# A cast queued behind a copy in the third feed-forward layer, and a pause ahead of the first state update in the linear attention

## The chip, the cores and the metric

The kernel runs on one core of a Trainium2 chip. The core has a matrix engine (PE, with PEld for its weight loads), a vector engine (DVE), a scalar engine (ACT), a general engine (POOL) and a synchronisation engine (SP) that here only issues transfers; POOL issues transfers too. Each engine works through its own queue of instructions in order, and semaphores hold an instruction back until what it needs is done. The metric is the time of one execution in microseconds (us).

## The reference

A trunk of four layers on 512 tokens of 1024 features, in fp32. Each layer is a mixer and a feed-forward network (FFN), each behind an RMS norm and added to the residual. The mixers are a state-space scan, a gated linear attention, a differential attention and the scan again. What matters here:

```python
def swiglu_ffn(h, w_gate_up, w_down):
    g, u = jnp.split(h @ w_gate_up, 2, axis=-1)
    return (jax.nn.silu(g) * u) @ w_down

# gla_mixer, chunks of 64 tokens, 4 heads
upd = jnp.einsum('bnchk,bnchv->bnhkv', k_dec, v)
decay = jnp.exp(tot)
def chunk_step(state, xs):
    dec_c, upd_c = xs
    state = dec_c[..., None] * state + upd_c
    return state, state
...
o = jnp.einsum('bnchk,bnhkv->bnchv', q, states)
o = o * lax.rsqrt(jnp.mean(o * o, axis=-1, keepdims=True) + NORM_EPS) * norm_g
```

The hidden width of the FFN is 2816.

## The kernel before

**Precision.** Each fp32 matrix is kept as a high part (a cast to fp32r on ACT, L420) and a low part (what the cast left, on DVE, L428); a product is three matmuls, high by high, high by low and low by high. The pair of a weight tile is `whl`, of which five exist; a new cast waits until the product that read the oldest pair is through.

**Seven products.** The gate-up matrix is worked in 11 blocks of 256 columns of each half (`b` 0 to 10). A block multiplies two 2 x 2 arrangements of quarters, and does so with seven products in place of eight. On the weight side the quarters are "11", "21" and "22", the sum "1" (quarters 12 + 11, to which "22" is added for product six and "21" for product four) and the sum "3" (quarters 12 + 22). The sums "1" and "3" are made by two loads: a plain one that SP issues, and an accumulating one that POOL issues behind it. The tiles of "11" and "3" come from a pool of three (`wst`). The order on PE in a block is product one (PSUM bank `a`), five (bank `c`), six (on top of `a`), two (bank `d`), seven (on top of `a`), three (on top of `c`), four (on top of `a`), 24 matmuls each (L594). Between them ACT copies a bank out before the next product adds to it: L796 (`one_out`, tile `r1`), L814 (`five_out`, tile `r5`), L828 (`six_out`, tile `r2`); DVE adds and subtracts (L803, L834, L841, L842), multiplies with the norm's factors (L768) and by the gate (L851); ACT takes the silu (L769) and casts the result to the activation pair (L861, low part on DVE, L862). L817 adds quarters into "1".

The blocks go in groups of four, four and three, and behind each group stands the down product (L448 to L450, evicted at L576). The first two blocks of a layer are interleaved by a written plan and have their "3" split early. From block 2 on, product seven splits "3" when it is emitted, through the helper `halves`. The layer index of the third FFN is 2, and it alone is built with `turn`, since its activations leave in the order that the scan behind it wants.

**Linear attention.** Its input projection is done in six such blocks. Blocks 0 and 1 are interleaved. From block 2 on, `block` takes a list of steps and runs one behind each of the seven products. With block 3 these are `later` (exponents of the suffix sums, `suf`) and then `core(0)`: for the first two heads, `updates` (L2261, eight matmuls into two banks, then copies or state steps on DVE, L2269 and L2271) and `readout` (L2284, eight matmuls; squares with their sum on ACT, L2290; epsilon on DVE, `ms`, L539; the root on POOL, `rs`, L541; the scaled output on DVE, L2298). A step of `core` holds a readout and the next pair of updates; the last holds a readout alone. Block 4 carries `core(1)` for the other two heads.

**What sets the order.** In the linear attention from block 2 on, PE keeps the written order and the other queues are ordered when the kernel is built, by the builder's scheduler. In the third FFN behind the first two blocks all queues are ordered by it. `issue_after(x)` gives the scheduler one more rule, without a semaphore: what is written inside it, and runs on the engine of `x`, is queued behind `x`.

## Time and profile before

| | us |
|---|---|
| median of three runs | 2259.27 |
| lowest and highest | 2256.43, 2262.32 |
| the profiled execution | 2255.34 |
| its span, from the first to the last instruction | 2253.6 |

The span is 1.7 us shorter than the profiled execution's own time. In the profile's rows a time is given from the start of the span. A row of the timeline has the start, the length, the engine, the line, the operation, the tile written and the tiles read, the shape and how many such instructions are merged; in brackets stands the idle time before it and what ended it. An instruction's length can overlap its neighbour's, so the spacing of starts is what counts for an engine that works without a gap. A matmul's tile is named without its number: `a`, `c` and `d` are the PSUM banks above, `op` a readout, `upd` an update, `work` the state.

### The profile page before, as it was taken

What the parts mean: (1) busy time and instruction counts of PE and PEld (TensorE: products, weight loads), DVE (VectorE), ACT (ScalarE), POOL (GpSimd) and SP (SyncE); (2) the same over time, 40 slices, a digit from 0 to 9 for tenths busy, and PEclk for the clock granted to TensorE, in tenths of its full rate; (3) what the DMA queues carried; (4) which work ended last, traced back from release to release, by engine and by line L of the source; (5) the groups of instructions that cost most, each with busy time, mean ns of one, the idle gap of its engine ahead of it and who ended that gap; (6) DMA issues with size and microseconds to landing.
All of it is one profiled execution on the core that took longest, in us unless ns stands there. A gap on an engine that the chain in (4) does not pass through costs nothing.

```text
span 2253.6 us, 38448 instructions
## 1 busy us (share of the span) xinstructions
PE 2174.0 (96%) x15415; PEld 1969.4 (87%) x15415; DVE 1637.0 (73%) x2495; ACT 1137.2 (50%) x1827; POOL 338.1 (15%) x447
## 2 busy tenths in 40 slices
PE   6999999999999999999999999999999899999998
PEld 5888979989988899999888888989998788989997
DVE  9955878786877598776745676967766965957675
ACT  8534645444655365564435775644444234635443
POOL 4301141431211010100002221101000000101000
PEclk9999999999999999999999999999999999999999
DMA  4356666774863667765337465975641546766632
GB/s 90 63 170 160 168 168 172 175 182 133 207 149 94 168 161 198 178 175 135 103 128 163 97 143 143 251 196 133 180 99 48 157 143 157 197 161 161 167 75 75
DMA packets 309180, 333.62 MB, mean 148 GB/s; under 512 B 70477, under 2 KB 253033, under 8 KB 308874
## 3 DMA queue, kind: packets, MB, share of 16 engines
q1 hardware_dynamic: 238970, 238.93, 35.0%
q0 software_dynamic: 70032, 92.23, 21.9%
q8 instruction: 121, 1.98, 0.4%
q14 instruction: 57, 0.47, 0.1%
HBM read 297.16 MB, written 18.75 MB: 140 GB/s over the span
## 4 chain that ended last, share of the span: by engine, by line
PE 79%; DVE 9%; ACT 5%; issue 4%; DMA 2%; SPq 1%; POOL 1%; DVEq 0%; POOLq 0%; ACTq 0%
PE a L594 20%; PE acc L448 11%; PE acc L450 11%; PE acc L449 11%; PE c L594 10%; PE d L594 5%; PE y L1620 2%; DVE whl L428 2%; ACT whl L420 1%; PE op L2586 1%; PE s L2553 1%; DMA wst<-in_ffn_w_down_dram 1%; PE tp L117 1%; PE V L1584 1%; PE acc L2641 1%
## 5 line engine op out<-in xcount | busy, mean ns | idle before, releaser
L428 DVE TENSOR_TENSOR whl<-wst,whl 128x1024 fp32r<-128x1024 f32 x260 | 316.8, 1223 | 217.0 <-ACT whl L420 214.3
L420 ACT CAST whl<-wst 128x1024 fp32r<-128x1024 f32 x260 | 272.1, 1051 | 264.8 <-PE acc L450 176.1
L594 PE MATMUL a<-side,whl 128*128 128x256 f32 x3240 | 392.1, 277 | 9.1 <-DVE whl L428 6.3
L594 PEld LDWEIGHTS a<-side,whl 128*128 128x128 f32 x3240 | 378.5, 188 | 11.8 <-DVE whl L428 7.4
L448 PE MATMUL acc<-whl,act 128*128 128x512 f32 x704 | 276.0, 392 | 2.0 <-DVE g L768 2.0
L449 PE MATMUL acc<-whl,act 128*128 128x512 f32 x704 | 274.4, 390 | 0.0
L450 PE MATMUL acc<-whl,act 128*128 128x512 f32 x704 | 274.4, 390 | 0.0
L594 PE MATMUL c<-side,whl 128*128 128x256 f32 x2160 | 260.9, 277 | 3.8 <-DVE whl L428 3.8
L594 PEld LDWEIGHTS c<-side,whl 128*128 128x128 f32 x2160 | 252.6, 188 | 4.7 <-DVE whl L428 4.6
L428 DVE TENSOR_TENSOR whl<-slot,whl 128x1024 fp32r<-128x1024 f32 x105 | 127.7, 1221 | 66.4 <-ACT whl L420 65.9
L448 PEld LDWEIGHTS acc<-whl,act 128*128 128x128 f32 x704 | 132.1, 188 | 31.3 <-DVE g L768 2.9
L450 PEld LDWEIGHTS acc<-whl,act 128*128 128x128 f32 x704 | 132.1, 188 | 27.7
L420 ACT CAST whl<-slot 128x1024 fp32r<-128x1024 f32 x105 | 110.0, 1052 | 90.8 <-PE acc L450 46.2
L449 PEld LDWEIGHTS acc<-whl,act 128*128 128x128 f32 x704 | 132.2, 188 | 26.1
L594 PE MATMUL d<-sides,whl 128*128 128x256 f32 x1080 | 132.3, 278 | 2.5 <-ACT whl L420 2.5
L594 PE MATMUL a<-sides,whl 128*128 128x256 f32 x1080 | 132.3, 278 | 1.9 <-DVE whl L428 1.2
L420 ACT CAST whl<-halves 128x1024 fp32r<-128x1024 f32 x87 | 91.3, 1053 | 83.9 <-DVE halves L817 33.6
L594 PEld LDWEIGHTS d<-sides,whl 128*128 128x128 f32 x1080 | 127.8, 188 | 3.3 <-ACT whl L420 3.3
L594 PEld LDWEIGHTS a<-sides,whl 128*128 128x128 f32 x1080 | 127.9, 188 | 3.2 <-DVE whl L428 1.4
L428 DVE TENSOR_TENSOR whl<-halves,whl 128x1024 fp32r<-128x1024 f32 x87 | 105.9, 1220 | 32.2 <-ACT whl L420 31.9
L759 POOL DMA_DIRECT2D wst<-in_ffn_w_gate_up_dram x44 | 57.2, 1299 | 437.9 <-DMA wst<-in_ffn_w_gate_up_dram 206.2
L861 ACT CAST act<-r 128x512 fp32r<-128x512 f32 (+1 forms) x110 | 66.2, 644 | 104.6 <-DVE r L842 84.1
(496 smaller groups left out, 4066.3 us busy)
## 6 DMA issues: line engine op xcount, KB each, us to landing
wst<-in_ffn_w_gate_up_dram SPq DMA_DIRECT2D x88, 512.0 KB, 4.7
wst<-in_ffn_w_down_dram SPq DMA_DIRECT2D x88, 512.0 KB, 4.5
slot<-in_ffn_w_gate_up_dram SPq DMA_DIRECT2D x69, 512.0 KB, 6.9
wst<-in_ffn_w_gate_up_dram POOLq DMA_DIRECT2D x44, 512.0 KB, 6.1
halves<-in_ffn_w_gate_up_dram SPq DMA_DIRECT2D x42, 512.0 KB, 6.3
wst<-in_s_w_glu_dram SPq DMA_DIRECT2D x32, 512.0 KB, 4.9
wst<-in_diff_w_qkv_dram SPq DMA_DIRECT2D x24, 512.0 KB, 4.4
slot<-in_ffn_w_gate_up_dram POOLq DMA_DIRECT2D x18, 512.0 KB, 9.3
```

The costliest lines, as they stand in the source:

```text
L117: tr.nc.tensor.transpose(p[:, j], h[:, j * P : (j + 1) * P], tr.ident[:])
L420: self.last["high"] = self.nc.scalar.copy(hl[:, 0], w[:])
L428: self.last["low"] = self.nc.vector.tensor_tensor(hl[:, 1], w[:], hl[:, 0].bitcast(F32), op=ALU.subtract)
L448: mm(out, lh, rh, start=first, stop=False)
L449: mm(out, lh, rl, start=False, stop=False)
L450: self.last["mm"] = mm(out, ll, rh, start=False, stop=last)
L594: mm(o, *two, start=first and not (j or k or n), stop=k == 3 and n == 2, skip_group_check=True,)
L759: nc.gpsimd.dma_start(w[:], left.quarter(*plus, b), accum_op=ALU.add)
L861: self.last["act high"] = nc.scalar.copy(dst[:, 0, j], src[:, j])
L1584: mm(V[kk][z][:, bs(b)], inm[:, z, bs(b)], U[:, bs(b)], start=True, stop=True)
L1620: mm(yb[:, b], q[:, j, b], om[:, j // 2, bs(b)], start=False, stop=j == 3)
L2553: nc.tensor.matmul(ss[m][:], qs[:, m, ts], ks[:, m, z], start=z == 0, stop=z == 1)
```

## The change

Two edits, of which neither adds or removes arithmetic.

In `five_out` the copy of bank `c` is remembered. In `seven`, for the layer with `turn` and where "3" is not split yet, the cast of "3" is written inside `issue_after` that copy, and the low part behind it; `product` then finds the pair ready. The cast can so no longer stand ahead of its block's L814 on ACT.

In the linear attention an empty step is put between `later` and `core(0)`, so each step of the first two heads' core stands one product later. The first updates stood behind product five and now stand behind six; the first readout, with the second updates, stood behind six and now stands behind two; and so on to the last readout, which stood behind three and now stands behind four.

```diff
         def five_out():
             keep["r5"] = T("r5")
-            nc.scalar.copy(keep["r5"][:], bank["c"][:])
+            keep["tie"] = nc.scalar.copy(keep["r5"][:], bank["c"][:])
...
         def seven():
+            if turn and "3" not in H:
+                with self.tc.issue_after(keep["tie"].ins):
+                    high("3")
+                low("3")
             product("3", "3", bank["a"], False)
...
             vs[1] = room("D", "v1")
-            block(3, Rows(vs[1]), (later, *core(0)))
+            block(3, Rows(vs[1]), (later, pause, *core(0)))
```

The queues, first ACT in the third FFN around block 3 (the last of the first group). Its tiles are `r1_15076`, `r5_15106` and `r2_15136`; `whl_15169` is the pair of "3", `whl_15197` that of "22", `whl_15227` that of "1" for product four, and `act_15030` belongs to block 2. Before:

```order
L420 COPY whl_15139<-halves_14131 128x1024
L769 ACTIVATE g2_15026<-g2_15026 128x512
L420 COPY whl_15169<-wst_15045 128x1024
L796 COPY r1_15076<-a_15048 128x512
L861 COPY act_15030<-r5_14865 128x64x4 x2
L420 COPY whl_15197<-gain_13547 128x1024
L814 COPY r5_15106<-c_15078 128x512
L420 COPY whl_15227<-halves_14131 128x1024
L828 COPY r2_15136<-a_15048 128x512
```

and in the change (its lines from 831 on have numbers higher by 4):

```order
L420 COPY whl_15139<-halves_14131 128x1024
L769 ACTIVATE g2_15026<-g2_15026 128x512
L796 COPY r1_15076<-a_15048 128x512
L865 COPY act_15030<-r5_14865 128x64x4 x2
L814 COPY r5_15106<-c_15078 128x512
L420 COPY whl_15169<-wst_15045 128x1024
L420 COPY whl_15197<-gain_13547 128x1024
L420 COPY whl_15227<-halves_14131 128x1024
```

The cast of "3" moves from the place ahead of L796 to the place behind L814, and with the cast of "22" and that of "1" it makes three casts in a row.

The same queue in a later block, 5, whose tiles are `r1_15780`, `r5_15810` and `r2_15840`; `whl_15873` is the pair of "3". Before:

```order
L420 COPY whl_15873<-wst_15749 128x1024
L769 ACTIVATE g2_15730<-g2_15730 128x512
L796 COPY r1_15780<-a_15752 128x512
L420 COPY whl_15901<-halves_14131 128x1024
L861 COPY act_15734<-r5_15582 128x64x4 x2
L814 COPY r5_15810<-c_15782 128x512
L420 COPY whl_15931<-slot2_14311 128x1024
L828 COPY r2_15840<-a_15752 128x512
```

and in the change:

```order
L769 ACTIVATE g2_15730<-g2_15730 128x512
L796 COPY r1_15780<-a_15752 128x512
L865 COPY act_15734<-r5_15582 128x64x4 x2
L814 COPY r5_15810<-c_15782 128x512
L420 COPY whl_15873<-wst_15749 128x1024
L420 COPY whl_15901<-halves_14131 128x1024
L420 COPY whl_15931<-slot2_14311 128x1024
```

Here too the three casts follow each other behind L814, and L828 follows them as before.

PE in block 3 of the linear attention, from product five on (`c_6867`; six, seven and four write `a_6821`). Before:

```order
L594 MATMUL c_6867<-whl_6868,side1_6010 128x256 x24
L2261 MATMUL upd_6897<-v0_6013,kd_6549 128x256
L2261 MATMUL upd_6898<-v0_6013,kd_6549 128x256
L2261 MATMUL upd_6897<-v0_6013,kd_6549 128x256
L2261 MATMUL upd_6898<-v0_6013,kd_6549 128x256
L594 MATMUL a_6821<-whl_6908,side2_6011 128x256 x24
L2284 MATMUL op_6937<-work_6503,qT_6017 64x256 x4
L2261 MATMUL upd_6950<-v0_6013,kd_6549 128x256
L2261 MATMUL upd_6951<-v0_6013,kd_6549 128x256
L2261 MATMUL upd_6950<-v0_6013,kd_6549 128x256
L2261 MATMUL upd_6951<-v0_6013,kd_6549 128x256
L594 MATMUL d_6960<-whl_6961,sides_5772 128x256 x24
```

and in the change:

```order
L594 MATMUL c_6867<-whl_6868,side1_6010 128x256 x24
L594 MATMUL a_6821<-whl_6898,side2_6011 128x256 x24
L2265 MATMUL upd_6927<-v0_6013,kd_6549 128x256
L2265 MATMUL upd_6928<-v0_6013,kd_6549 128x256
L2265 MATMUL upd_6927<-v0_6013,kd_6549 128x256
L2265 MATMUL upd_6928<-v0_6013,kd_6549 128x256
L594 MATMUL d_6937<-whl_6938,sides_5772 128x256 x24
L2288 MATMUL op_6967<-work_6503,qT_6017 64x256 x4
L2265 MATMUL upd_6980<-v0_6013,kd_6549 128x256
L2265 MATMUL upd_6981<-v0_6013,kd_6549 128x256
L2265 MATMUL upd_6980<-v0_6013,kd_6549 128x256
L2265 MATMUL upd_6981<-v0_6013,kd_6549 128x256
```

Product six moves ahead of the first updates, and product two ahead of the first readout. On POOL the first root stays ahead of one accumulating load and the other roots behind it, as before.

## The prediction

> **What bounds the kernel now.** I read the page first, then the chain that ended last, then the timelines of the two places that the change touches.

> ```profile
> span 2253.6 us, 38448 instructions
> PE 2174.0 (96%) x15415; PEld 1969.4 (87%) x15415; DVE 1637.0 (73%) x2495; ACT 1137.2 (50%) x1827; POOL 338.1 (15%) x447
> ```

> TensorE is busy for 96% of the span. An edit of order can therefore gain only where PE waits at the two places, and it can lose wherever it makes PE wait. The first place is block 3 of the linear attention. Its PE rows, with the wait in brackets:

> ```profile
> 661.38 1.14 PE L2261 MATMUL upd<-v,kd 64*128 64x256 f32 x8
> ...
> 665.39 1.08 PE L2284 MATMUL op<-work,qT 128*64 128x256 f32 x8
> 666.40 1.13 PE L2261 MATMUL upd<-v,kd 64*128 64x256 f32 x8
> ...
> 670.47 1.83 PE L2284 MATMUL op<-work,qT 128*64 128x256 f32 x8
> 672.23 1.13 PE L2261 MATMUL upd<-v,kd 64*128 64x256 f32 x8
> ...
> 676.31 0.65 PE L2284 MATMUL op<-work,qT 128*64 128x256 f32 x2
> 679.36 1.08 PE L2284 MATMUL op<-work,qT 128*64 128x256 f32 x6 [2.40 <-DVE work L2271]
> 680.36 1.13 PE L2261 MATMUL upd<-v,kd 64*128 64x256 f32 x8
> ...
> 684.45 0.65 PE L2284 MATMUL op<-work,qT 128*64 128x256 f32 x2
> 685.83 1.08 PE L2284 MATMUL op<-work,qT 128*64 128x256 f32 x6 [0.73 <-DVE work L2271]
> 686.83 3.09 PE L594 MATMUL a<-whl,side 128*128 128x256 f32 x24
> ...
> 692.68 1.13 PE L2261 MATMUL upd<-v,kd 64*128 64x256 f32 x8
> ```

> A readout (`op`) that waits for nothing takes 1.01 from its start to the next row (665.39 to 666.40). The next three take 1.76, 4.05 and 2.38, so they lose 0.75, 3.04 and 1.37, together 5.16 us. They wait for the state steps of DVE (L2271), and DVE waits in its turn for POOL:

> ```profile
> 668.44 0.16 DVE L539 TENSOR_SCALAR ms<-ms 128x2 f32<-128x2 f32 x1
> ...
> 669.51 0.87 DVE L2298 SCALAR_TENSOR_TENSOR on<-op,rs,ng 128x256 f32<-128x256 f32 x2 [0.52 <-POOL rs L541]
> ...
> 677.64 0.88 DVE L2298 SCALAR_TENSOR_TENSOR on<-op,rs,ng 128x256 f32<-128x256 f32 x2 [3.71 <-POOL rs L541]
> 678.44 1.25 DVE L2271 SCALAR_TENSOR_TENSOR work<-work,dec,upd 128x256 f32<-128x256 f32 x3
> ...
> 688.00 0.16 DVE L539 TENSOR_SCALAR ms<-ms 128x2 f32<-128x2 f32 x1
> ...
> 689.87 0.88 DVE L2298 SCALAR_TENSOR_TENSOR on<-op,rs,ng 128x256 f32<-128x256 f32 x2 [0.58 <-POOL rs L541]
> ```

> On POOL the second root (L541) stands behind an accumulating load, and that one waits for a plain load, which the chain names:

> ```profile
> 675.54 1.33 POOL L626 DMA_DIRECT2D wst<-in_gla_w_in_dram  x1 [6.07 <-DMA wst<-in_gla_w_in_dram]
> ...
> 683.39 0.70 POOL L541 TENSOR_TENSOR rs<-ms,mhalf 128x2 f32<-128x2 f32 x1 [5.78 <-DVE ms L539]
> 688.24 1.60 POOL L541 TENSOR_TENSOR rs<-ms,mhalf 128x2 f32<-128x2 f32 x1 [4.16 <-DVE ms L539]
> ```

> ```profile
> 668.55 6.34 DMA wst<-in_gla_w_in_dram
> ```

> The second place is block 3 of the third FFN, the last of its first group; PE, then ACT:

> ```profile
> 1472.96 2.99 PE L594 MATMUL c<-side,whl 128*128 128x256 f32 x24
> 1477.62 3.09 PE L594 MATMUL a<-side,whl 128*128 128x256 f32 x24 [1.68 <-ACT r L796]
> 1480.55 2.97 PE L594 MATMUL d<-sides,whl 128*128 128x256 f32 x24
> 1484.40 3.01 PE L594 MATMUL a<-side,whl 128*128 128x256 f32 x24 [0.87 <-ACT r L828]
> ```

> ```profile
> 1476.04 1.04 ACT L420 CAST whl<-wst 128x1024 fp32r<-128x1024 f32 x1 [3.15 <-PE c L594]
> 1476.99 0.58 ACT L796 COPY r<-a 128x512 f32<-128x512 f32 x1
> ...
> 1482.81 1.05 ACT L420 CAST whl<-halves 128x1024 fp32r<-128x1024 f32 x1 [2.87 <-DVE halves L817]
> 1483.77 0.58 ACT L828 COPY r<-a 128x512 f32<-128x512 f32 x1
> ```

> Product six may not write bank a before ACT has copied product one out of it (L796). That copy stands behind the cast of the summed weights "3". The row puts the cast's wait down to PE, but the program also has it wait for its load, which was issued on POOL and took 11.5 us:

> ```profile
> 1464.48 1.28 POOL L759 DMA_DIRECT2D wst<-in_ffn_w_gate_up_dram  x1 [4.48 <-DVE whl L428]
> ```

> ```profile
> wst<-in_ffn_w_gate_up_dram POOLq DMA_DIRECT2D x1, 512.0 KB, 11.5
> ```

> So it landed at 1475.98, and 1476.04 is the start that follows. A cast that is needed two products later holds up a copy that is needed at once.

> **The cast, part by part.** No instruction is added or taken away. In blocks 3 to 10 the cast of "3" moves on ACT behind L814 (on DVE its low part moves with it, and the silu, the copies and the activation casts move ahead). Blocks 0 to 2 keep their order.

> In block 3, product one ends near 1473.1 (five starts at 1472.96), and L796 (0.58) is then done by 1473.8. Product six starts when five lets it, at most 2.93 after 1472.96 (1477.62 to 1480.55 is that spacing), so near 1475.8 and not at 1477.62: 1.8 gained. The cast of "3" follows L814, at 1476.5, after the landing. The activation casts ahead of it no longer delay DVE, so the sum for "4" is ready at 1477.4, its cast runs at about 1478.4, and L828 at 1479.4. Two starts at 1478.7 and seven at 1481.5, with L828 done at 1480.0: the second wait goes too. Seven starts 2.9 earlier than 1484.40. The casts' low parts are done by 1478.8, 1480.0 and 1481.1, ahead of seven, three (1484.3) and four (1487.0). **Term: -2.9.** Its bounds are -2.9 (no wait left) and 0 (another wait in the same place).

> In blocks 4 to 10, PE has no wait to lose. One block, by PE and DVE:

> ```profile
> 1558.35 2.88 PE L594 MATMUL c<-side,whl 128*128 128x256 f32 x24
> ...
> 1566.55 2.88 PE L594 MATMUL a<-side,whl 128*128 128x256 f32 x24
> ...
> 1571.99 2.88 PE L594 MATMUL a<-side,whl 128*128 128x256 f32 x24
> ```

> ```profile
> 1566.76 0.68 DVE L803 TENSOR_TENSOR r<-r,d 128x512 f32<-128x512 f32 x1
> ...
> 1570.47 0.68 DVE L834 TENSOR_TENSOR r<-r,a 128x512 f32<-128x512 f32 x1
> ```

> Five ends at 1561.23. Behind it ACT now runs L814 (about 0.5 to the next start), three casts 0.95 apart (1476.04 to 1476.99), and L828, done near 1565.2; seven needs that copy at 1566.55, so 1.3 is spare. DVE gets the first low part at 1562.8 and then has four lows at 1.14 to 1.22 each, so L803 slips from 1566.76 to 1567.4 or 1567.7. L834 slips by as much, from its end at 1571.15 to 1571.8 or 1572.1; four needs it at 1571.99. So I cost the seven blocks at **0** (cover: 0.2 by the shorter spacing; by the longer, 0.1 a block, +0.7, is lost). The buffer of "3" comes free later by an estimated 4 us (its low part moves from ahead of L814 to 1562.8 and after), and so do the next load into it on SP and the loads queued behind that. They are for a later block or for the down product, a block's length or more ahead of their casts. Cost 0; with the cover gone, up to that 4 us once a group.

> **The pause, part by part.** Every update and readout of the first core moves one product later on PE; the last readout now stands behind block 3's last product. Six starts at 661.4 and the first update at 664.4. The low that frees the `wst` buffer comes a little sooner on DVE, so SP's load starts an estimated 0.4 before 668.55; 6.34 later it lands at 674.5, and the accumulate occupies POOL until 676.5 (2.0 from landing to end, as 674.89 to 676.87). With products at 2.95 to 3.0 (686.83 to 692.68 holds two), updates at 1.1 and a readout at 1.01, the second readout comes after product seven at 673.5, and its root is asked for at 677.2: POOL is free, by 0.7. From `ms` to L2298 I take 1.07 (668.44 to 669.51), then 0.79 for two L2298 and 1.25 for three steps:

> - second readout: steps end at 673.8, it would end at 674.5 anyway, loss 0;
> - third: `ms` 677.2, steps end 680.3, next row 0.67 later (679.69 to 680.36) at 680.9, loss 1.35;
> - fourth: `ms` 682.1 with a low right behind it, as at 688.00, where the root took 1.60 and L2298 came 1.87 after `ms`; four steps then end at 686.4, next row at 687.1, loss 1.1.

> The losses shrink from 5.16 to 2.45. **Term: -2.7**, and the update at 692.68 comes at 690.0. Bounds: -5.2 (no loss left) and 0 (same losses); I take the value that follows from the rows, in the middle. [...]

> **Sum.** -2.9 - 2.7 + 0 = -5.6 us. Against the profiled execution's own 2255.34 us that is 2249.7; the median of the runs shown is 3.9 above it, so the forecast for the median is 2259.27 - 5.6 = 2253.7, or -0.25%. What comes behind both places (loads, silus, sums) is released by PE, DVE or ACT rows that move along, so I let the gain reach the end.

> **The rivals.**

> 1. *Only one half pays.* If SP's load or the accumulate lands a microsecond later, the second root stands behind it again and the readouts lose as before: 2259.27 - 2.9 = 2256.4. If block 3 of the FFN finds another wait: 2256.6. For it: both rest on landings (6.34 and 11.5 us). Against: 0.7 of room at the first, and the copies no longer depend on the second.
> 2. *All waits go.* -5.16 - 2.9 = -8.1, 2251.2. Against: DVE's own chain (root, two L2298, three steps) is 3.1 long and starts only behind a readout.
> 3. *Slower: the three casts in a row make DVE late for product four.* The place is L834 in blocks 4 to 10. With 0.2 spare and a lateness w, seven blocks lose 7 x (w - 0.2). The gain is eaten at w = 1.0, and the run is slower by over 6.8 us from w = 2.0. The longest wait of DVE for ACT near here is the 3.03 at 1478.15 below; at that price, 7 x 2.8 = 19.8, the time is 2259.27 - 5.6 + 19.8 = 2273.5. Against: DVE has idle time in each block, and nothing in these blocks waits for a landing.

> ```profile
> 1478.15 1.18 DVE L862 TENSOR_TENSOR act<-r,act 128x256 fp32r<-128x256 f32 x2 [3.03 <-ACT act L861]
> ```

> **How the numbers follow.** 0.3% is 6.8 us, about what a measurement of this kernel can tell from no change: the three runs shown span 5.9. The forecast has 0.68, rival 1 has 0.15, rival 2 has 0.08, rival 3 has 0.09. The forecast lies 1.2 us on the near side of the -0.3% mark (2252.5), and a median moves by more than that, so a third or more of its 0.68 falls beyond: 0.25. Faster: 0.25 + 0.08 = 0.33. Slower: 0.07, the part of rival 3 beyond w = 2.0. Same: the remaining 0.60. The range goes from rival 2 less the 2.8 by which the lowest run lies under its median, 2248, to rival 1 plus the 3.0 of the highest, rounded up to 2260.

> **What would show it.** In the changed profile, product six of block 3 of the third FFN should have no wait for L796, and seven none for L828; the products of blocks 4 to 10 should still follow each other at 2.72. In the linear attention the second readout should lose nothing, the third and fourth about 1.3 and 1.1, with the second root not behind POOL's load; and from that readout to the next core's first update nothing else should move. I am wrong if PE shows waits for L834 or L828 in blocks 4 to 10, if DVE again waits 3 us for a root, or if PE's gain at either place comes back as a wait in the down product or the output product behind it.

## The result, and the profile after

| | us |
|---|---|
| kernel before, median of 6 runs | 2258.87 |
| kernel after, median of 6 runs (2245.59 to 2250.25) | 2249.36 |
| ratio, with its 95% interval | 0.9959 (0.9948 to 0.9969) |
| profiled execution, before and after | 2255.34 and 2249.67 |

By the medians the change saves 9.5 us, by the two profiled executions 5.7. The forecast was 2253.7, from a sum of -5.6. So the two profiles agree with the sum to 0.1 us and the medians do not. Most of the experiments ask which of the two is the change.

The totals of the profile after show little, since PE is still busy all the time:

```profile
span 2248.0 us, 38450 instructions
PE 2174.6 (97%) x15415; PEld 1971.6 (88%) x15415; DVE 1635.6 (73%) x2495; ACT 1138.7 (51%) x1827; POOL 341.1 (15%) x447
```

The timeline of PE in block 3 of the linear attention, after (L2265 is the update and L2288 the readout; lines from 831 on are higher by 4):

```profile
668.74 1.08 PE L2288 MATMUL op<-work,qT 128*64 128x256 f32 x8
...
673.84 1.08 PE L2288 MATMUL op<-work,qT 128*64 128x256 f32 x8
674.85 1.14 PE L2265 MATMUL upd<-v,kd 64*128 64x256 f32 x8
678.94 0.65 PE L2288 MATMUL op<-work,qT 128*64 128x256 f32 x2
680.33 1.08 PE L2288 MATMUL op<-work,qT 128*64 128x256 f32 x6 [0.74 <-DVE work L2275]
681.34 1.14 PE L2265 MATMUL upd<-v,kd 64*128 64x256 f32 x8
685.70 1.86 PE L2288 MATMUL op<-work,qT 128*64 128x256 f32 x8 [0.29 <-DVE work L2275]
687.49 3.09 PE L594 MATMUL a<-whl,sides 128*128 128x256 f32 x24
690.51 1.14 PE L2265 MATMUL upd<-v,kd 64*128 64x256 f32 x8
```

A readout without a wait takes 1.01 to the next row. The second now does (673.84 to 674.85) and loses nothing. The third takes 2.40 and loses 1.39. For the fourth, product three would end near 685.40 (681.34 plus 1.07 for the updates and 2.99 for the product), and the next row begins at 687.49: a loss of 1.08. Before, the second root stood directly behind the accumulating load, whose own start at 675.54 came 2.2 us behind the `ms` of that root (673.39):

```profile
676.37 1.24 POOL L541 TENSOR_TENSOR rs<-ms,mhalf 128x2 f32<-128x2 f32 x1
```

After, that load stands between the roots and holds none of them up:

```profile
671.38 0.72 POOL L541 TENSOR_TENSOR rs<-ms,mhalf 128x2 f32<-128x2 f32 x1 [4.17 <-DVE ms L539]
675.64 1.33 POOL L626 DMA_DIRECT2D wst<-in_gla_w_in_dram  x1 [3.55 <-DMA wst<-in_gla_w_in_dram]
677.87 0.71 POOL L541 TENSOR_TENSOR rs<-ms,mhalf 128x2 f32<-128x2 f32 x1 [0.89 <-DVE ms L539]
682.75 1.60 POOL L541 TENSOR_TENSOR rs<-ms,mhalf 128x2 f32<-128x2 f32 x1 [4.16 <-DVE ms L539]
```

Block 3 of the third FFN, after, PE and then ACT:

```profile
1470.62 2.99 PE L594 MATMUL c<-side,whl 128*128 128x256 f32 x24
1473.45 2.99 PE L594 MATMUL a<-side,whl 128*128 128x256 f32 x24
1476.27 2.95 PE L594 MATMUL d<-sides,whl 128*128 128x256 f32 x24
1479.06 2.88 PE L594 MATMUL a<-side,whl 128*128 128x256 f32 x24
```

```profile
1470.82 0.59 ACT L796 COPY r<-a 128x512 f32<-128x512 f32 x1 [0.26 <-PE a L594]
...
1473.65 0.59 ACT L814 COPY r<-c 128x512 f32<-128x512 f32 x1 [0.81 <-PE c L594]
1474.61 1.05 ACT L420 CAST whl<-wst 128x1024 fp32r<-128x1024 f32 x1 [0.38 <-DMA wst<-in_ffn_w_gate_up_dram]
```

Both waits of PE are gone. The cast still waits for its landing, 0.38 us, and now the row itself names the load; but no copy that PE needs at once stands behind it.

Set beside each other along PE, the two executions are 0.48 us apart (after the later) at the suffix sums of block 3 in the linear attention and -2.17 at the second core's first update: -2.65. At product five of block 3 in the third FFN they are -2.34 apart and at product seven -5.34: -3.0. Code that the change does not touch moves too. The start-up stage came out 2.0 us shorter in the execution after, but its granted clock was 0.50 for 3.4 us from 293.54 and again from 648.53, where the execution before ran at 1.00; that cost it about 1.5 and 1.6 us. What the two executions differ by outside of the two places adds up to about zero by chance.

### The profile page after: what moved, and what is told of

Same layout as the page of the kernel before. It is cut to its first block, busy times and chain, and to the rows that moved or that the text cites. A ratio compares the mean times of both kernels' runs of the same rounds, so it can differ in the third digit from the quotient of the medians.

```text
span 2248.0 us, 38450 instructions
## 1 busy us (share of the span) xinstructions
PE 2174.6 (97%) x15415; PEld 1971.6 (88%) x15415; DVE 1635.6 (73%) x2495; ACT 1138.7 (51%) x1827; POOL 341.1 (15%) x447
## 4 chain that ended last, share of the span: by engine, by line
PE 81%; DVE 8%; ACT 4%; issue 3%; DMA 1%; SPq 1%; POOL 0%; DVEq 0%; POOLq 0%; ACTq 0%
PE a L594 20%; PE acc L448 11%; PE acc L450 11%; PE acc L449 11%; PE c L594 10%; PE d L594 5%; PE y L1624 2%; DVE whl L428 2%; ACT whl L420 1%; PE op L2590 1%; PE V L1588 1%; PE s L2557 1%; PE tp L117 1%; PE acc L2645 1%; DMA wst<-in_ffn_w_down_dram 1%
## 5 line engine op out<-in xcount | busy, mean ns | idle before, releaser
L428 DVE TENSOR_TENSOR whl<-wst,whl 128x1024 fp32r<-128x1024 f32 x260 | 316.8, 1223 | 224.5 <-ACT whl L420 223.4
L420 ACT CAST whl<-wst 128x1024 fp32r<-128x1024 f32 x260 | 272.1, 1051 | 256.3 <-PE acc L450 164.6
L594 PE MATMUL a<-side,whl 128*128 128x256 f32 x3240 | 392.5, 277 | 6.7 <-DVE whl L428 6.3
L594 PEld LDWEIGHTS a<-side,whl 128*128 128x128 f32 x3240 | 379.0, 188 | 9.0 <-DVE whl L428 7.3
L594 PE MATMUL c<-side,whl 128*128 128x256 f32 x2160 | 261.3, 277 | 3.5 <-DVE whl L428 3.5
L594 PEld LDWEIGHTS c<-side,whl 128*128 128x128 f32 x2160 | 253.0, 188 | 4.4 <-DVE whl L428 4.3
L428 DVE TENSOR_TENSOR whl<-slot,whl 128x1024 fp32r<-128x1024 f32 x105 | 127.6, 1221 | 60.7 <-ACT whl L420 60.7
L420 ACT CAST whl<-slot 128x1024 fp32r<-128x1024 f32 x105 | 109.9, 1053 | 86.3 <-PE acc L450 46.3
L594 PE MATMUL d<-sides,whl 128*128 128x256 f32 x1080 | 132.3, 278 | 2.5 <-ACT whl L420 2.5
L594 PE MATMUL a<-sides,whl 128*128 128x256 f32 x1080 | 132.6, 279 | 1.6 <-DVE whl L428 1.2
L594 PEld LDWEIGHTS d<-sides,whl 128*128 128x128 f32 x1080 | 127.9, 188 | 3.3 <-ACT whl L420 3.3
L594 PEld LDWEIGHTS a<-sides,whl 128*128 128x128 f32 x1080 | 128.2, 188 | 2.8 <-DVE whl L428 1.4
L428 DVE TENSOR_TENSOR whl<-halves,whl 128x1024 fp32r<-128x1024 f32 x87 | 105.8, 1221 | 30.7 <-ACT whl L420 30.4
L420 ACT CAST whl<-halves 128x1024 fp32r<-128x1024 f32 x87 | 91.0, 1051 | 70.6 <-DVE halves L817 26.0
L759 POOL DMA_DIRECT2D wst<-in_ffn_w_gate_up_dram x44 | 57.2, 1299 | 448.7 <-DMA wst<-in_ffn_w_gate_up_dram 144.5
## 6 DMA issues: line engine op xcount, KB each, us to landing
wst<-in_ffn_w_gate_up_dram SPq DMA_DIRECT2D x88, 512.0 KB, 4.6
wst<-in_ffn_w_down_dram SPq DMA_DIRECT2D x88, 512.0 KB, 4.6
slot<-in_ffn_w_gate_up_dram SPq DMA_DIRECT2D x69, 512.0 KB, 6.2
wst<-in_ffn_w_gate_up_dram POOLq DMA_DIRECT2D x44, 512.0 KB, 6.1
halves<-in_ffn_w_gate_up_dram SPq DMA_DIRECT2D x42, 512.0 KB, 6.5
wst<-in_s_w_glu_dram SPq DMA_DIRECT2D x32, 512.0 KB, 4.9
wst<-in_diff_w_qkv_dram SPq DMA_DIRECT2D x24, 512.0 KB, 4.4
slot<-in_ffn_w_gate_up_dram POOLq DMA_DIRECT2D x18, 512.0 KB, 9.2
```

The costliest lines, as they stand in the source:

```text
L420: self.last["high"] = self.nc.scalar.copy(hl[:, 0], w[:])
L428: self.last["low"] = self.nc.vector.tensor_tensor(hl[:, 1], w[:], hl[:, 0].bitcast(F32), op=ALU.subtract)
L594: mm(o, *two, start=first and not (j or k or n), stop=k == 3 and n == 2, skip_group_check=True,)
L759: nc.gpsimd.dma_start(w[:], left.quarter(*plus, b), accum_op=ALU.add)
```

## The experiments

Each kernel was timed against the kernel before on one chip. "Before" and "after" here are the two kernels of the change.

### Each half alone, and the two kernels again

The first kernel has the FFN's edit alone, the second the pause alone, as the diff shows them. The other two are the kernels before and after without an edit.

The cast alone:

> The cast's edit alone, the linear attention as before. My theory (the copies stood behind a cast that waits for its landing): in block 3 of the third FFN product six and product seven lose their waits, -2.9 us in the trace at product seven, and -2.9 in the median. The rival that the landings scatter (typical executions of the kernel before stall longer there than its profiled one): -2.9 in the trace at most places, but -4 to -6 in the median. The rival that the rest of the measured 9.5 us comes from blocks 4 to 10: product one of block 10 stands further ahead than product seven of block 3 does, by 1 us or more. The rival that the rest is scatter of stages that the change leaves alone: the median is anywhere from -6 to 0 with an interval that holds -2.9.

The pause alone:

> The pause alone, the third FFN as before. My theory (the root stood behind the accumulating load on POOL, and one product later it does not): -2.7 us at the first update of the second pair of heads, -2.7 in the median; the readouts lose 0, 1.4 and 1.1. The rival that landings scatter: -4 to -7 in the median, with the same -2.7 in a trace. The two medians added give -5.6 by my theory and -9.5 if it is the edits that bring the rest.

The kernel before, against itself:

> The kernel before against itself: 0 in the median, with an interval that shows what the comparison can tell. Its profile is a second one of the same code. By my theory product seven of block 3 again loses 2.5 us in waits and the readouts 5.2, within 0.3, and a difference in span comes from elsewhere. By the rival that landings scatter, one of the two sums is longer by 1 us or more.

The kernel after, again:

> Both edits again: my theory says -5.6 us in the median, the first measurement said -9.5 with an interval from -11.7 to -7.0. If it comes near -9.5 again the forecast lacks a term of 4 us; if it comes near -5.6 the first comparison had drawn slow executions of the kernel before.

| kernel | median, us | before, us | ratio (95% interval) |
|---|---|---|---|
| cast alone | 2252.83 | 2257.09 | 0.9982 (0.9973 to 0.9991) |
| pause alone | 2252.77 | 2257.09 | 0.9984 (0.9975 to 0.9993) |
| before again | 2256.81 | 2257.09 | 0.9999 (0.9990 to 1.0008) |
| after again | 2250.64 | 2257.09 | 0.9973 (0.9963 to 0.9983) |

The whole change gives -6.1 us by its ratio here and not -9.5. The halves give -4.1 and -3.6 by their ratios, each with an interval of about 2 us to both sides, which holds the forecast terms. Their sum is -7.7, so a further gain from the two edits together is not needed.

The second profile of the kernel before found what its first had not shown. The cast of "3" on ACT, then PE, then the windows with their granted clock (the first of the last three numbers):

```profile
1474.31 1.04 ACT L420 CAST whl<-wst 128x1024 fp32r<-128x1024 f32 x1 [3.59 <-DMA wst<-in_ffn_w_gate_up_dram]
1475.26 0.58 ACT L796 COPY r<-a 128x512 f32<-128x512 f32 x1
```

```profile
1470.49 2.88 PE L594 MATMUL c<-side,whl 128*128 128x256 f32 x24
1475.89 4.63 PE L594 MATMUL a<-side,whl 128*128 128x256 f32 x24 [2.52 <-ACT r L796]
1480.36 2.93 PE L594 MATMUL d<-sides,whl 128*128 128x256 f32 x24
1483.13 2.88 PE L594 MATMUL a<-side,whl 128*128 128x256 f32 x24
```

```profile
core 0: us, PE busy (x) PEld busy (x) DVE busy (x) ACT busy (x) POOL busy (x), PEclk, DMA share, GB/s
1473.40:1475.90 2.50, 0.01 (x1) 0.01 (x1) 0.00 (x0) 1.59 (x3) 0.00 (x0) 1.00 0.87 137
1475.90:1477.00 1.10, 1.10 (x7) 1.10 (x8) 0.58 (x2) 1.10 (x3) 0.00 (x0) 0.77 1.19 191
1477.00:1479.50 2.50, 2.50 (x14) 2.50 (x13) 2.50 (x4) 1.18 (x2) 0.00 (x0) 0.50 0.03 4
1479.50:1481.00 1.50, 1.50 (x13) 1.50 (x13) 1.47 (x2) 0.00 (x0) 0.00 (x0) 0.86 0.64 171
```

The load landed later: the cast starts 3.82 us behind product five where it was 3.08, and the row names the load as what it waited for. The wait for L796 is 2.52 where it was 1.68, and behind it product six ran at a granted clock of 0.50. It takes 4.47 to the next product in place of 2.93. Product seven shows no wait for L828 in this execution, since product six, slower, ends later. In all the same code lost 1.1 us more at this place.

### The FFN's edit, by blocks

```diff
-            if turn and "3" not in H:
+            if turn and b == 3 and "3" not in H:
```

and the other with `b > 3`. Both without the pause.

In block 3 alone:

> The cast is queued behind the copy in block 3 of the third FFN alone; blocks 4 to 10 and the linear attention as before. My theory (only block 3 waits for a landing): all of the cast's gain is here, -2.8 to -4.2 us at product seven of block 3 and about -4 in the median, as with the whole edit (2252.8 against 2257.1). The rival that blocks 4 to 10 bring part of it: half of that or less.

In blocks 4 to 10 alone:

> The cast is queued behind the copy in blocks 4 to 10 alone. My theory: 0, within +-2 us, the waits at products six and seven of block 3 as in the kernel before (2.5 us and more), no wait in blocks 4 to 10. The rival that the three casts in a row make DVE late for product four: +1 to +7 and waits of product four. The rival that these blocks gain: -1 to -2.

Measured were 0.9983 (0.9974 to 0.9992; 2252.31 against 2256.75) for block 3 alone, and 1.0002 (0.9993 to 1.0011; 2257.18) for blocks 4 to 10 alone. Block 3 carries the whole gain; the seven other blocks are worth nothing that can be measured, as the forecast had costed them. In the profile with blocks 4 to 10 alone, block 3 waits as before:

```profile
1473.09 2.99 PE L594 MATMUL c<-side,whl 128*128 128x256 f32 x24
1478.29 3.10 PE L594 MATMUL a<-side,whl 128*128 128x256 f32 x24 [2.21 <-ACT r L796]
1481.23 2.97 PE L594 MATMUL d<-sides,whl 128*128 128x256 f32 x24
1485.08 3.09 PE L594 MATMUL a<-side,whl 128*128 128x256 f32 x24 [0.87 <-ACT r L828]
```

### POOL's load behind the root, without the pause

```diff
             if plus:
-                nc.gpsimd.dma_start(W[name][:], left.quarter(*plus, b), accum_op=ALU.add)
+                root = getattr(self, "second_root", None) if name == "3" and b == 5 else None
+                with self.tc.issue_after(root.ins) if root else nullcontext():
+                    nc.gpsimd.dma_start(W[name][:], left.quarter(*plus, b), accum_op=ALU.add)
...
                 r_ = self.rsqrt(ms[:], 2, 1e-6)
+                if (hf, t) == (0, 1):
+                    self.second_root = self.last_pow
```

On POOL two neighbours change places, and nothing else moves on any queue.

> The kernel before, with one move: on POOL the accumulating load for block 5 stands behind the second root of the linear attention instead of ahead of it; no pause, no cast edit. My theory (the root waits for the place in POOL's queue): the second root starts with its ms, about 3 us sooner, DVE's wait of 3.7 falls to 0.5, the third readout loses 0 to 0.6 instead of 3.0, the second still 0.75 and the fourth 1.4; -2.4 to -3.0 us in all. The rival that the pause gains by giving the chain of state steps more time, and the load's place does not matter: 0. The rival that the load's later place costs: block 5 or the output product behind it waits, +1 or more.

The ratio is 0.9983 (0.9974 to 0.9991), the median 2254.01 against 2256.75. POOL, then DVE, then PE at the third readout (lines here are 2 higher than before, and 4 higher from the root's call on, as L2302 for L2298):

```profile
674.70 0.69 POOL L541 TENSOR_TENSOR rs<-ms,mhalf 128x2 f32<-128x2 f32 x1 [4.17 <-DVE ms L539]
676.28 1.34 POOL L628 DMA_DIRECT2D wst<-in_gla_w_in_dram  x1 [0.90 <-DMA wst<-in_gla_w_in_dram]
```

```profile
674.45 0.17 DVE L539 TENSOR_SCALAR ms<-ms 128x2 f32<-128x2 f32 x1
...
675.42 0.88 DVE L2302 SCALAR_TENSOR_TENSOR on<-op,rs,ng 128x256 f32<-128x256 f32 x2 [0.43 <-POOL rs L541]
```

```profile
677.26 1.08 PE L2286 MATMUL op<-work,qT 128*64 128x256 f32 x8
678.28 1.13 PE L2263 MATMUL upd<-v,kd 64*128 64x256 f32 x8
```

The wait of 3.71 became 0.43 and the third readout loses nothing where it lost 3.04. This stretch gains 3.3 us in the profile, more than it does with the pause. So the wait was the load's place in POOL's queue. The pause is one way round it, and the move is the direct one. The timed runs are too few to set against the 3.3: the medians differ by 2.7, the ratio gives 3.8 (2.0 to 5.9), and both the stretch and the pause lie within that. In this profile 0.8 us was lost again in block 3 of the third FFN, where the wait was 2.10 and product six again ran at a clock near 0.50.

### State steps ahead of the scaled output

```diff
-                    steps.append(lambda t=t: (readout(hf, t), updates(hf, t + 1)))
+                    steps.append(lambda t=t: (updates(hf, t + 1), readout(hf, t)))
```

This was tried on the kernel after; then with the moved load too; then with the cast's edit and the moved load but without the pause. A fourth kernel has the cast's edit and the moved load alone, and a fifth is the kernel after as a control.

On the kernel after:

> The changed kernel with one move more: in each step of the two cores the next pair of updates is written ahead of the readout, so that on DVE the four state steps stand ahead of the scaled output (which waits for the root) and not behind it. My theory (what the pause leaves, 1.4 and 1.1 us, and 0.7 in the other core, is the chain readout, root, scaled output, state steps): the readouts wait for nothing, -2.5 to -3.2 us against the changed kernel, so about -9 against the kernel before. The rival that the state steps wait for DVE's other work ahead of them: the losses stay, -6. The rival that the updates, now sooner, wait for their PSUM banks: slower than the changed kernel.

With the moved load, with the pause:

> The changed kernel with the moved load and with the updates written ahead of the readouts. Its earlier form without the moved load was no faster than the changed kernel, and DVE waited 3.6 us for a root behind the accumulating load. My theory: that wait alone ate the gain; with the load behind the second root the wait is 0.5, and the time is 2 to 3 us below the changed kernel's. The rival that the order of steps itself costs (updates that wait for their banks): no faster than the changed kernel.

With the moved load, without the pause:

> As the kernel with the cast's edit and the moved load, and the updates written ahead of the readouts; no pause. My theory: with the root free of POOL's load, DVE never waits 3 us in the middle of its queue, and the state steps no longer follow the root: the readouts' losses of 5.2 us fall to 1 or less and the other core's 0.7 goes, so -8 to -9 against the kernel before and -2 against the changed kernel. The rival that the steps wait for DVE's casts and sums ahead of them: losses of 2 to 3 remain, -6.

The cast's edit and the moved load alone:

> The cast's edit with the moved accumulating load in place of the pause. My theory: the two places do not touch each other, so the separately measured gains add: -3.3 at the first update of the second core, -2.8 to -4.2 in the third FFN, -6 to -7.5 in all, level with the changed kernel or up to 0.6 us faster. The rival that the two gains overlap somewhere behind (a stage bound by its loads): -4.

The control:

> The changed kernel on the same chip, as the control of the three: -6 to -6.5 us against the kernel before, as in the second comparison (2250.6 against 2257.1); the first comparison's -9.5 would be outside of what is measured again.

| kernel | median, us | ratio to before (95% interval) |
|---|---|---|
| steps first, on the kernel after | 2250.17 | 0.9971 (0.9960 to 0.9982) |
| steps first, moved load, pause | 2249.35 | 0.9963 (0.9950 to 0.9977) |
| steps first, moved load, no pause | 2247.29 | 0.9955 (0.9942 to 0.9968) |
| moved load, no pause | 2248.86 | 0.9966 (0.9954 to 0.9978) |
| control: the kernel after | 2251.01 | 0.9971 (0.9960 to 0.9982) |

The first of them brought nothing that can be measured, against the expectation: the builder put POOL's load ahead of the first root this time. DVE waited for that root with the next state steps queued behind its wait, and PE waited for them:

```profile
680.99 0.88 DVE L2302 SCALAR_TENSOR_TENSOR on<-op,rs,ng 128x256 f32<-128x256 f32 x2 [3.61 <-POOL rs L541]
682.56 1.65 DVE L2275 SCALAR_TENSOR_TENSOR work<-work,dec,upd 128x256 f32<-128x256 f32 x4
```

```profile
683.48 1.91 PE L2265 MATMUL upd<-v,kd 64*128 64x256 f32 x8 [1.01 <-DVE work L2275]
```

With the load tied behind the second root and no pause, every readout of the first core follows its product with no loss at all. The last two, to be set beside the 2.40 and the 1.79 of the kernel after:

```profile
679.93 1.08 PE L2290 MATMUL op<-work,qT 128*64 128x256 f32 x8
680.95 3.09 PE L594 MATMUL c<-whl,side 128*128 128x256 f32 x24
683.97 1.08 PE L2290 MATMUL op<-work,qT 128*64 128x256 f32 x8
684.98 3.01 PE L594 MATMUL a<-whl,side 128*128 128x256 f32 x24
```

It is the fastest of all kernels here, 9.6 us below the kernel before. Against the kernel after on the same chip (five and seven runs) the medians are 3.7 apart, with an interval from 1.0 to 6.4. With the pause kept, or with the move alone, the difference to the kernel after (1.7 and 2.2 by the medians) is within its interval; for the first, 2 to 3 us had been expected. Whether the pause itself costs something once the load is moved is not shown: the two kernels' times overlap, and their profiles are alike at both places (the table below).

### The two places in all profiles

From the starts of PE's rows in each profile, in us: "sums to core" goes from the first matmul of the suffix sums to the second core's first update; "five to three" goes from product five to product three of block 3 in the third FFN.

| kernels | sums to core | five to three |
|---|---|---|
| before | 37.65 | 14.29 |
| before again | 36.97 | 15.36 |
| cast alone; block 3 alone | 37.87; 37.13 | 11.16; 11.14 |
| blocks 4 to 10 alone | 37.82 | 14.91 |
| pause alone | 34.91 | 14.03 |
| after, three profiles | 35.00, 34.92, 34.92 | 11.16, 10.92, 10.92 |
| moved load; with the cast's edit | 34.39; 34.17 | 15.08; 10.92 |
| steps first, on the kernel after | 35.06 | 10.92 |
| steps first, moved load, pause | 32.48 | 10.92 |
| steps first, moved load, no pause | 32.32 | 10.92 |

With the waits, five to three takes 14.03 to 15.36 (five profiles, mean 14.73). Without them it takes 10.92 to 11.16. The mean difference is 3.7, and the execution on which the forecast was made lies near the low end with 14.29. Sums to core takes 36.97 to 37.87 without the pause or the moved load (five, mean 37.49) and 34.91 to 35.00 with the pause and neither the moved load nor the other order of steps (four, mean 34.94): 2.55. The two add to 6.3.

## Why the prediction was right, and where not

**The cast, -2.9.** Right in kind and place: product six waited for L796 only because the cast of "3" stood ahead of it and waited for its landing, and the kernel with the edit in block 3 alone carries all of the gain. The size was read from one execution. The profile after gives -3.0 at product seven; over all profiles the place is worth 3.7, because the landing comes earlier or later (the wait for L796 was 1.54, 1.68, 2.10, 2.21 and 2.52 in the five profiles that have it) and because the granted clock dropped to 0.50 behind two of these waits (2.10 and 2.52). The stated bound of -2.9 (no wait left) was therefore no bound: it treated one execution's wait as the wait. This is the term that was mis-sized.

**The pause, -2.7.** Right step by step: losses of 0, 1.35 and 1.1 were forecast for the three readouts; 0, 1.39 and 1.08 were measured. The fourth root is slow, 1.60 beside 0.71, with the low part of a cast right behind its `ms` (DVE, 682.50 and 682.57), as the forecast took from 688.24; what makes it slow there no run shows. POOL was free 0.9 ahead of the second `ms`; 0.7 had been worked out. Over all profiles the stretch gives 2.55. What the forecast took as given is that POOL's load has to stand ahead of the second root; moved behind it, the same wait is gone without a pause.

**Blocks 4 to 10, 0.** Right: 1.0002 (0.9993 to 1.0011) when they alone are changed. No product of these blocks waits in the profile after. The cover was larger than the 0.2 that had been worked out: in the block that the prediction shows, L838 (L834 before) ends at 1566.07, and product four starts at 1566.53.

```profile
1565.39 0.68 DVE L838 TENSOR_TENSOR r<-r,a 128x512 f32<-128x512 f32 x1
...
1566.53 2.88 PE L594 MATMUL a<-side,whl 128*128 128x256 f32 x24
```

**The rivals.** That only one half pays, and that the three casts make DVE late, are both refuted by the runs of the halves and of blocks 4 to 10. That all waits go is not what the change does (1.39 and 1.08 are left), but it is what the fastest kernel does in the linear attention.

**The time and the chances.** The forecast of 2253.7 was 4.3 above the measured median, inside its range. Part of that lies in the base: 2259.27 was the median of three runs, and the other comparisons give 2257.09, 2256.75 and 2256.88 for the kernel before. The two later comparisons of the whole change give -6.45 and -5.87 us by their medians, ratios 0.9973 and 0.9971. All 89 timed runs of the kernel before have a median of 2256.8 and all 21 of the kernel after 2250.3, so about -6.6. The forecast sum of -5.6 falls short of that by 1.0, of which the two places as all profiles have them explain 0.7 (6.3 against 5.6). The -9.5 of the first comparison was not found again; that few runs draw so far apart is the likely reason, not a shown one. That the two profiled executions agree with the sum to 0.1 us is luck: the shared code differs by up to 2 us between them and only happens to cancel. The chance of 0.33 for faster by over 0.3% was low beside the first comparison's -0.41%, and fair beside -0.27% and -0.29%: the change lies on that mark.

## What to carry to other kernels

A wait for a landing that stands in an in-order queue ahead of a copy or a root is paid by whatever is queued behind it: at the copy PE waited 1.54 to 2.52 us, and behind the root the third readout lost 3.04. Look first for the one neighbour that can change places with it, before giving the chain more time elsewhere: in the profiles here, two rows of POOL were worth more than a pause of a whole product (34.39 us from sums to core against 34.91). Size such a gain from several profiles of the kernel before, since the same wait came out anywhere from 1.54 to 2.52 us. Look at the order again after each edit, since a later one can make the builder put the load back.

## What the runs showed of the hardware

The price of a wait of PE was not only its length. Of ten waits of 1.5 to 2.6 us at the two places, four were followed by a granted clock of 0.50 (behind 2.10, 2.52, 2.52 and 2.55); six were not (1.54, 1.68, 2.00, 2.16, 2.21 and 2.40). With the drop, product six in the FFN took 4.47 and 4.46 us to the next row, beside 2.93 without it, and in the linear attention the six matmuls of the third readout and the next updates took 3.69 (679.04 to 682.73, cast alone), beside 2.07 (677.97 to 680.04, before again): 1.5 to 1.6 us more. Part of the price came back: in these three cases the next wait (for L828, or at the fourth readout) was gone. At the place as a whole the profiles with a drop are 0.8 us longer in the FFN (15.22 against 14.41) and 0.6 in the linear attention (37.85 against 37.25). One of the four is shown above. Behind the wait of 2.21 the matmuls ran at a granted clock of 1.00 (14 in 1.71 us):

```profile
1478.29:1480.00 1.71, 1.71 (x14) 1.71 (x15) 1.18 (x3) 1.71 (x3) 0.00 (x0) 1.00 1.00 158
```

```profile
645.00:648.50 3.50, 3.50 (x34) 3.50 (x33) 2.01 (x3) 0.00 (x0) 0.25 (x1) 1.00 0.50 162
648.53:651.94 3.41, 3.41 (x17) 3.41 (x17) 0.00 (x0) 2.07 (x3) 1.00 (x1) 0.50 0.51 65
```
